# Experts of a routed layer with a fixed plan of blocks in place of branches

## The chip, the cores and the metric

The program runs on one core of one Trainium2 chip. The metric is the time of one execution on the device in microseconds (us), as a median over runs. The engines are named as in the profile: PE is TensorE (matmuls; PEld is its weight load), DVE is VectorE, ACT is ScalarE, POOL is GpSimd, SP is SyncE, which here does nothing but issue transfers.

## The reference, cut to what matters

The layer mixes 2048 tokens (attention and a convolution), then routes each token to two of 32 experts, and ends with a gated embedding. The change lies in the experts:

```
def expert_block(args):
    xb, e = args                                  # 128 rows of one expert
    hdn = jax.nn.silu(xb @ w1[e]) * (xb @ w3[e])  # 1024 -> 512
    return hdn @ w2[e]                            # 512 -> 1024
```

w1 and w3 are 1024 x 512, w2 is 512 x 1024, all in float32. How many rows an expert gets is known only once the router has run.

## The kernel before, in words

Every float32 operand of a large matmul is taken in two parts, high and low (`split`, L91 to L93): ACT copies the high part, a second engine subtracts it from the whole. A product is then three matmuls: high by high, high by low, low by high (`mm3`, L95 to L99). For a block of at most 64 rows the two parts of the rows lie side by side in one 128-column operand, so that two matmuls do (`both`, L1127).

The weights of an expert come in 12 pieces of 128 x 1024 (`unit`, L1080): SP loads a piece into `eraw` (9 buffers), ACT writes `ewh` and DVE or POOL `ewl` (15 buffers each). Pieces 0 to 3 serve the first half of the hidden columns (w1 and w3), 4 to 7 the second half, 8 to 11 are w2. `pull(n)` (L984) puts the next n pieces into the program; how many come at which place of an expert is written out in `PULLS`, 12 in all, and pieces 2, 6 and 10 are subtracted on POOL.

`pick` (L892) orders the experts by the number of their rows, large and small ones in turn, and writes for each of the 32 places which expert it is, its number of rows and of blocks. `moe` (L964) walks over the 32 places. Each has a first block of 128 rows, and what further blocks it has is settled by branches on the number of rows: none up to 128, a 64-row block up to 192, otherwise a 128-row block and more (`many`, L1001). A block: its rows are gathered by POOL (`gather`, L1092), transposed by PE and split (`turned`, L1100), multiplied with w1 and w3 (`products`, L1139, tile `ups`), gated (`gated`, L1164: silu on ACT, product on DVE), the hidden half transposed and split (`turn`, L1173, tiles `hps` and `hh`), multiplied with w2 (`down`, L1182, tile `yd`), copied and scattered by POOL. The second block of a place is set between the halves of the first. After the experts, `ple` (L1239) reads the scattered rows and makes the last products (tile `gps`) with 12 more pieces, pulled during the last expert.

Inside `moe` the order of instructions on each engine is that of the program (`manual_schedule`, L1022); nothing is moved by the compiler there.

Of the kernel before, what the change touches and what calls it, by code (L numbers as in the profile page):

```python
# [9 lines left out]
F32 = mybir.dt.float32  # L10
# [35 lines left out]
MOE_W = (9, 15)  # L46
POOL_UNITS = (2, 6, 10)
PULLS = (1, 1, 1, 2, 3, 2, 2)
# [3 lines left out]
HALF_FEW = 5  # L52
XT1_AT = 0
# [5 lines left out]
LEAD = (2, 200)  # L59

# [19 lines left out]
def AGAIN(nc, out, ps, sb):  # L80
    nc.gpsimd.tensor_copy(out, sb)


class K:
# [49 lines left out]
    def keep(self):  # L134
        """What lasts from the merge to the end."""
        cp = self.ctx.enter_context(self.tc.tile_pool(name="keep", bufs=1, reuse_waits="tile"))
        self.gl = cp.tile([P, NT, NG], F32, name="gl")
        self.nc.vector.memset(self.base, 0.0)
        self.dst = cp.tile([P, NBLK * NE], I32, name="dst")
        self.idx = cp.tile([P, NBLK * NE], I32, name="idx")  # L140
        self.slots = cp.tile([1, 3, NE], I32, name="slots")
        self.xp = self.ctx.enter_context(self.tc.tile_pool(name="xp", bufs=2, reuse_waits="tile"))

    def consts(self, cp):
# [24 lines left out]
        # brings in the table of the square root  # L169
# [383 lines left out]
    def attn_probs(self, h, g, Qt, Kt):  # L553
        """Unnormalized p0 - lam * (sum p0 / sum p1) * p1; what is missing, 1 / sum p0, goes into s0."""
# [262 lines left out]
    def route(self, q, L):  # L817
# [12 lines left out]
        def first(vals, top, k):  # L830
            """One-hot of the first place that holds the maximum."""
# [60 lines left out]
    def pick(self):  # L892
# [48 lines left out]
        V.tensor_copy(self.slots, vp[:1, :3, :])  # L941

# [1 line left out]
    def projected(self, t, pt, w, pool, tag, o):  # L944
        """Tile t of it, from units of [128, 1024] in two parts."""
# [9 lines left out]
    def project(self, parts):  # L955
        """The first half of the tiles, while the table is made."""
# [7 lines left out]
    def moe(self):  # L964
# [8 lines left out]
        self.ed = ctx.enter_context(tc.tile_pool(name="ed", bufs=2, space=PSUM, reuse_waits="tile"))  # L973
        engines = [ET.PE, ET.Activation, ET.DVE, ET.Pool, ET.SP]
        col = lambda t, e, b: t[:, b * NE + e : b * NE + e + 1]
        val = lambda i, e, lo, hi, eng=engines: nc.values_load(self.slots[0:1, i, e : e + 1], engines=eng, min_val=lo, max_val=hi)

        def rows(e, b):
            return self.gather(col(self.idx, e, b)) if e < NE else None

        W, src = {}, []
        self.last = W

        def pull(n, after=None):  # L984
            for _ in range(n):
                i = sum(len(w) for w in W.values())
                e, c = i // 12, i % 12
                if e > NE:
                    return
                if c == 0:  # L990
                    W[e] = []
                    if e == NE:
                        src[:] = halves(A["wpp"]) + halves(A["pT"][1]) + [A["wpg"][c, i] for c in range(2) for i in range(4)]
                    elif e:
                        i = val(0, e, 0, NE - 1, [ET.SP])
                        src[:] = [A["we"][bass.ds(i, 1), c] for c in range(12)]
                    else:
                        src[:] = [A["we"][0, c] for c in range(12)]
                W[e].append(self.unit(src[c], nc.gpsimd if c in POOL_UNITS else nc.vector, after))

        def many(e, w, n, xt, fill):  # L1001
            g = self.ep.tile([P, D], F32, name="g", tag="y")
            self.gather(col(self.idx, e, 2), g)
            self.block(w, xt, col(self.dst, e, 1), fill)
            with tc.If(n > 2 * P):
                self.turned(g, True, xt[3])
                with tc.If(n > 2 * P + FEW) as full:
                    self.block(w, xt, col(self.dst, e, 2), y=g)
                    with tc.If(n > 3 * P):
                        with tc.For_i(3, val(2, e, 0, NBLK), 1) as i:  # L1010
                            b = i * NE + e
                            self.gather(self.column(self.idx, b, "ix"), g)
                            self.block(w, self.turned(g, True, xt[3]), self.column(self.dst, b, "dx"), y=g)
                with full.Else():
                    self.block(w, xt, col(self.dst, e, 2), y=g, few=True)

        self.ctx.enter_context(tc.manual_schedule(engines={ET.SP}))
        xt, xt1 = (self.turned(x, more=i == 1) for i, x in enumerate(self.first))
        pull(EARLY)
        pull(12 - EARLY, self.gathered)  # L1020
        xs0 = rows(1, 0)
        with tc.manual_schedule(engines=set(engines)):  # L1022
            for e in range(NE):
                w = W[e]
                h0 = self.gated(self.raised(w, xt, 0, self.ups("eu")), "hd")
                u1 = self.ups("eu")
                fill = lambda i: self.products(w, xt, 1, u1, 0, i)
                pull(PULLS[0])
                n = val(1, e, 0, S)
                with tc.If(n > P) as more:  # L1030
                    if e % 2:
                        x = self.ep.tile([P, D], F32, name="g", tag="y")
                        xt1 = self.turned(self.gather(col(self.idx, e, 1), x), more=True)
                    with tc.If(n > P + FEW) as full:  # L1034
                        many(e, w, n, xt1, fill)
                    with full.Else():
                        self.block(w, xt1, col(self.dst, e, 1), fill, few=True)
                with more.Else():
                    for i in range(2):
                        fill(i)  # L1040
                def also(at):
                    nonlocal xt1
                    if e % 2 and e + 1 < NE and at == XT1_AT:
                        xt1 = self.turned(xs1, more=True)

                def between(n):
                    pull(PULLS[5 + n])
                    if n == 0:
                        also(3)

                t0 = self.turn(h0, self.halves())
                pull(PULLS[1])
                self.products(w, xt, 1, u1, 1, 0)
                also(0)
                self.products(w, xt, 1, u1, 1, 1)
                h1 = self.gated(u1, "hd")
                pull(PULLS[2])
                yd = self.yds()
                self.down(w, yd, 0, 0, t0)
                also(1)  # L1060
                t1 = self.turn(h1, self.halves())
                pull(PULLS[3])
                self.down(w, yd, 0, 1, t0)
                if e + 1 < NE:
                    xt = self.turned(xs0)
                also(2)
                xs0 = rows(e + 2, 0)
                if e % 2 == 0:
                    xs1 = rows(e + 2, 1)
                pull(PULLS[4])  # L1070
                self.lowered(w, yd, t1, col(self.dst, e, 0), pull=between)
                if e == 0:
                    pull(MOE_W[1] - 12 - PULLS[0])

# [5 lines left out]
    def unit(self, src, lo_eng=None, after=None):  # L1080
        """A [128, 1024] piece of a weight matrix in two parts."""
# [18 lines left out]
    def turned(self, x, more=False, into=None):  # L1100
        """The transpose of a [128, 1024] tile in two parts, [128, 8, 128] each; `more`: the high part of 64 rows
# [274 lines left out]
```

## Time and profile before

| what | us |
|---|---|
| median of 3 runs | 2954.33 |
| lowest and highest run | 2951.59, 2961.68 |
| span of the profiled execution, first to last instruction | 2960.1 |
| first matmul of the experts | 1727.9 |
| first matmul of the last stage's projection | 2712.6 |

The profiled execution has its span as its own time; what lies around a span is not listed, and the span lies inside the range of the runs. The experts take about a third of it. PE is busy for 92% of the span, DVE 69%, ACT 50%, POOL 24%; these shares are means over stages that have little in common.

### The profile page before, as it was taken

To read this page: it belongs to the slowest core of one execution; us is meant where nothing else is said; L and a number is where in the kernel's file an instruction comes from. 1 tells how busy PE (TensorE), PEld (TensorE's weight loads), DVE (VectorE), ACT (ScalarE), POOL (GpSimd) and SP (SyncE) were. 2 spreads that over 40 slices of the span, in tenths; PEclk is the share of its full clock that TensorE was granted. 3 is DMA by queue.
4 is the path that set the end of the run, shared out by engine and by line. 5 is a ranking of instruction groups with operands and counts; after the bars stand their busy time and mean duration, and the time that the engine had idled before them with its cause. 6 is when DMAs were issued, how large, how long until landed. Compare 5 with 4: busy or idle time off the path is not lost. (4 is left out here: it accounts for less than half of the span.)

```text
span 2960.1 us, 40065 instructions
## 1 busy us (share of the span) xinstructions
PE 2736.7 (92%) x14078; PEld 2282.7 (77%) x14078; DVE 2041.7 (69%) x2860; ACT 1474.9 (50%) x2712; POOL 722.3 (24%) x463
## 2 busy tenths in 40 slices
PE   7999999999999999999999989898888989888988
PEld 5888877997778788787898867676666767666776
DVE  6995249995878888657567456666667777776564
ACT  4233352335766667544444345555455656565443
POOL 2021130123111000001101134544335444452122
PEclk9999999999999999999999989999999999999999
DMA  5134443235243331456556366777767776876371
GB/s 189 60 107 142 159 147 104 93 114 196 81 132 89 104 112 53 160 184 214 168 170 206 122 238 243 265 287 259 252 223 274 276 283 236 293 274 244 125 246 56
DMA packets 180220, 531.52 MB, mean 180 GB/s; under 512 B 19185, under 2 KB 48641, under 8 KB 179361
## 3 DMA queue, kind: packets, MB, share of 16 engines
q1 hardware_dynamic: 135536, 397.02, 39.9%
q0 software_dynamic: 25904, 92.45, 8.5%
q10 hardware_dynamic: 18432, 37.76, 3.4%
q8 instruction: 177, 2.90, 0.4%
q14 instruction: 171, 1.39, 0.1%
HBM read 424.66 MB, written 102.50 MB: 178 GB/s over the span
## 5 line engine op out<-in xcount | busy, mean ns | idle before, releaser
L93 DVE TENSOR_TENSOR ewl<-eraw,ewh 128x1024 fp32r<-128x1024 f32 x365 | 597.2, 1665 | 94.4 <-ACT ewh L92 88.5
L92 ACT ACTIVATE ewh<-eraw 128x1024 fp32r<-128x1024 f32 x464 | 474.1, 1065 | 54.0 <-PE mps L98 24.9
L387 DVE SCALAR_TENSOR_TENSOR co<-cb,pvt,co 128x1024 f32<-128x1024 f32 x240 | 313.6, 1345 | 1.6
L93 POOL TENSOR_TENSOR ewl<-eraw,ewh 128x1024 fp32r<-128x1024 f32 x99 | 253.8, 2563 | 185.4 <-ACT ewh L92 183.0
L1146 PE MATMUL ups<-ewh,xt 128*128 128x512 f32 x592 | 250.0, 422 | 40.3 <-issue 38.6
L1147 PE MATMUL ups<-ewl,xt 128*128 128x512 f32 x592 | 244.5, 413 | 0.9 <-DVE ewl L93 0.5
L97 PE MATMUL ps<-uh,wh 128*128 128x512 f32 x576 | 232.0, 405 | 4.4 <-ACT uh L92 4.4
L586 DVE TENSOR_REDUCE nm<-sc 128x1 f32<-128x512 f32 (+3 forms) x320 | 185.3, 606 | 66.1 <-PE sc L583 51.6
L98 PE MATMUL ps<-ul,wh 128*128 128x512 f32 x576 | 227.9, 397 | 1.1 <-POOL ul L93 1.1
L99 PE MATMUL ps<-uh,wl 128*128 128x512 f32 x576 | 227.2, 396 | 0.0
L1146 PEld LDWEIGHTS ups<-ewh,xt 128*128 128x128 f32 x592 | 119.0, 201 | 71.9 <-issue 46.0
L97 PE MATMUL ps<-wh,uh 128*128 128x384 f32 x512 | 173.0, 338 | 0.0
L99 PE MATMUL ps<-wh,ul 128*128 128x384 f32 x512 | 172.1, 336 | 0.0
L98 PE MATMUL ps<-wl,uh 128*128 128x384 f32 x512 | 172.0, 336 | 0.0
L1144 PE MATMUL ups<-ewh,xt 128*128 128x512 f32 x592 | 167.5, 406 | 3.7 <-issue 3.7
L97 PE MATMUL mps<-ewh,mh 128*128 128x256 f32 x512 | 150.3, 294 | 4.1 <-ACT mh L92 4.1
L403 POOL DMA_DIRECT2D G<-sg x64 | 35.1, 549 | 457.3 <-ACT sg L402 325.2
L98 PE MATMUL mps<-ewl,mh 128*128 128x256 f32 x512 | 145.8, 285 | 0.0
L99 PE MATMUL mps<-ewh,ml 128*128 128x256 f32 x512 | 145.2, 285 | 0.0
L1147 PEld LDWEIGHTS ups<-ewl,xt 128*128 128x128 f32 x592 | 119.3, 202 | 25.5 <-DVE ewl L93 1.0
L430 POOL TENSOR_TENSOR qn<-qk,qk_std 128x1024 f32<-128x1024 f32 x16 | 44.6, 2785 | 380.7 <-DVE qk_std L189 363.8
L1204 POOL DMA_INDIRECT Y<-y,dst x48 | 72.3, 1507 | 266.3 <-POOLq L1034 188.3
(340 smaller groups left out, 7238.5 us busy)
## 6 DMA issues: line engine op xcount, KB each, us to landing
eraw<-in_we SPq DMA_DIRECT2D x384, 512.0 KB, 7.3
G<-sg POOLq DMA_DIRECT2D x64, 256.0 KB, 2.7
eraw<-in_wac SPq DMA_DIRECT2D x32, 512.0 KB, 4.3
ga<-G SPq DMA_DIRECT2D x32, 512.0 KB, 5.1
eraw<-in_wo SPq DMA_DIRECT2D x32, 512.0 KB, 3.7
ys<-Y SPq DMA_DIRECT2D x32, 512.0 KB, 8.2
wraw<-in_wqkv SPq DMA_DIRECT2D x16, 768.0 KB, 4.2
wraw<-in_wg SPq DMA_DIRECT2D x20, 512.0 KB, 3.9
```

The lines of the kernel that those rows point to most:

```text
L92: nc.scalar.activation(hi, x, AF.Copy)
L93: (lo_eng or nc.vector).tensor_tensor(lo, x, f32(hi), ALU.subtract)
L97: nc.tensor.matmul(ps, lh, rh, start=start, stop=False)
L98: nc.tensor.matmul(ps, lh, rl, start=False, stop=False)
L99: nc.tensor.matmul(ps, ll, rh, start=False, stop=stop)
L387: nc.vector.scalar_tensor_tensor(acc, cb[:, i : i + HALF], wi, acc, ALU.mult, ALU.add)
L430: nc.gpsimd.tensor_tensor(qn.rearrange("p t (s d) -> p t s d", d=HD), qk.rearrange("p t (s d) -> p t s d", d=HD), r.unsqueeze(3).to_broadc ...
L586: nc.vector.tensor_reduce(nm[:, qi, m, c : c + 1], sc[:, :w], AX.X, ALU.max, negate=True)
L1144: self.nc.tensor.matmul(ps, xt[1][:, k, :], wk[0], start=False, stop=k == NK - 1)
L1146: self.nc.tensor.matmul(ps, xt[0][:, k, :], wk[0], start=k == 0, stop=False)
L1147: self.nc.tensor.matmul(ps, xt[0][:, k, :], wk[1], start=False, stop=False)
L1204: nc.gpsimd.indirect_dma_start(out=self.Y[:, :], out_offset=bass.IndirectOffsetOnAxis(ap=dst[R], axis=0), in_=y[R], in_offset=None)
```

## The change

A list `PLAN` says for each place in the order by rows which blocks it gets: five places two blocks of 128 rows (one of them a further 64), eleven 128 and 64, nine 128, seven 64. The blocks are put into the program without branches. An expert with more rows than its place holds is done once more, all its blocks, in a loop behind the others (`rest`), whose weights are loaded and split there for each block; `pick` writes a flag and, per place, the number of blocks to be redone. The order of PE's work is now written in steps: `X` transposes rows, `U(j, f, g)` is half `g` of the product for hidden half `f`, `T` turns a hidden half, `DN` is the product with w2. In a place with two blocks the steps of both are interleaved. Weight pieces are no longer pulled at fixed places: `did` keeps a count of PE's and DVE's time and pulls from that, and `U` and `DN` pull whatever they need that is not there yet. All pieces are subtracted on DVE; the buffers of `ewh` and `ewl` are 14 each.

```diff
-MOE_W = (9, 15)
-POOL_UNITS = (2, 6, 10)
-PULLS = (1, 1, 1, 2, 3, 2, 2)
+MOE_W = (9, 14)
+FULL, PART = P, FEW
+PLAN = [[FULL, FULL], [FULL, FULL, PART]] + [[FULL, FULL]] * 3 + [[FULL, PART]] * 11 + [[FULL]] * 9 + [[PART]] * 7
+SLOTS = [PLAN[s // 2 if s % 2 == 0 else NE - 1 - s // 2] for s in range(NE)]
+UNIT_US = 1.25
...
+        def pull(after=None):
+            nonlocal pulled, dve
...
+            W[e].append(self.unit(src[c], None, after))
+            pulled += 1
+            dve = max(dve, pe) + UNIT_US
+
+        def did(us):
+            nonlocal pe
+            pe += us
+            while dve <= pe and pulled < 12 * NE + 12 and (pulled < MOE_W[1] or pulled - MOE_W[1] in last):
+                pull()
+
+        def small(us):
+            nonlocal dve
+            dve = max(dve, pe) + us
...
+        def X(j):
...
+            j.xt = self.turned(j.x, j.few)
+            rows(j.k + 2)
+            small(0.64 if j.few else 1.28)
+            did(0.5 if j.few else 0.87)
+
+        def U(j, f, g):
+            while pulled <= 12 * j.e + 4 * f + 2 * g + 1:
+                pull()
...
+            if j.ends:
+                for c in range(2):
+                    last[12 * j.e + 4 * f + 2 * g + c] = True
+            if g == 1:
+                j.h = self.gated(j.u, j.few)
+                small(1.1 if j.few else 0.4)
+            did(1.82 if j.few else 2.72)
+
+        def T(j):
+            j.ht = self.turn(j.h, j.few)
+            small(0.4)
+            did(0.2)
+
+        def DN(j, f):
+            while pulled <= 12 * j.e + 8 + 2 * f + 1:
+                pull()
...
+                did(0.91 if j.few else 1.36)
...
+            for i, g in enumerate(groups):
+                nxt = groups[i + 1][0] if i + 1 < len(groups) else None
+                a = g[0]
+                X(a)
+                U(a, 0, 0)
+                held()
+                held = lambda: None
+                if len(g) == 2:
+                    b = g[1]
+                    X(b)
+                    U(a, 0, 1)
+                    U(b, 0, 0)
+                    T(a)
+                    a0 = a.ht
+                    U(b, 0, 1)
+                    U(a, 1, 0)
+                    T(b)
+                    b0 = b.ht
+                    U(a, 1, 1)
+                    a.ht = a0
+                    DN(a, 0)
+                    U(b, 1, 0)
+                    T(a)
+                    U(b, 1, 1)
+                    b.ht = b0
+                    DN(b, 0)
+                    X(nxt)
+                    T(b)
+                    DN(a, 1)
+                    DN(b, 1)
+                else:
+                    U(a, 0, 1)
+                    if nxt and not (a.few and nxt.few):
+                        X(nxt)
+                    U(a, 1, 0)
+                    T(a)
+                    U(a, 1, 1)
+                    DN(a, 0)
+                    X(nxt)
+                    T(a)
+                    held = lambda a=a: DN(a, 1)
+            held()
+            while pulled < 12 * NE + 12:
+                pull()
+            self.rest()
```

`last` holds the pieces whose last reader is already in the program. `gated` follows the second half of a product at once; `held` puts the last step of a place with one block behind the first step of the next place. Outside the experts, `ple` no longer has POOL copy 64 rows of every second tile, and `pick` gains 32 memsets and five small operations on DVE.

## Rows read from the trace of the kernel before

**Rows 1.** View by stretches; after the engines: granted clock, DMA share, GB/s.

```profile
core 0: us, PE busy (x) PEld busy (x) DVE busy (x) ACT busy (x) POOL busy (x), PEclk, DMA share, GB/s
...
1728.00:2708.00 980.00, 867.69 (x3800) 674.63 (x3801) 668.43 (x630) 550.90 (x800) 423.99 (x228) 0.94 0.73 262
```

**Rows 2.** PE's waits, 1728 to 2708 us: total, times, longest.

```profile
PE ups L1146 <- issue: 38.6, 16, 3.3
PE ups L1130 <- issue: 32.1, 11, 3.5
...
PE ups L1146 <- ACT ewh L92: 1.6, 1, 1.6
```

**Rows 3.** Groups by line and form, 1720 to 2720 us.

```profile
L93 DVE TENSOR_TENSOR ewl<-eraw,ewh 128x1024 fp32r<-128x1024 f32 x297 | 514.2, 1767 | 48.1 <-ACT ewh L92 42.3
L92 ACT ACTIVATE ewh<-eraw 128x1024 fp32r<-128x1024 f32 x396 | 402.4, 1067 | 2.5 <-DMA eraw<-in_we 2.3
L93 POOL TENSOR_TENSOR ewl<-eraw,ewh 128x1024 fp32r<-128x1024 f32 x99 | 253.8, 2563 | 185.4 <-ACT ewh L92 183.0 <-ACTq L1030 1.4
L1146 PE MATMUL ups<-ewh,xt 128*128 128x512 f32 x592 | 250.0, 422 | 40.3 <-issue 38.6 <-ACT ewh L92 1.6
...
L1131 PE MATMUL ups<-ewl,xt 128*64 128x512 f32 x192 | 84.4, 462 | 3.8 <-issue 3.8
```

**Rows 4.** Timeline of PE, 2333 to 2381 us: start, length, instruction, [idle before].

```profile
2333.74 1.08 PE L1144 MATMUL ups<-ewh,xt 128*128 128x512 f32 x4
2334.65 0.39 PE L97 MATMUL yd<-ewh,hh 128*128 128x512 f32 x1
2334.88 0.39 PE L98 MATMUL yd<-ewl,hh 128*128 128x512 f32 x1
...
2336.02 0.38 PE L1177 MATMUL hps<-cst,hd 128*128 128x128 f32 x2
...
2337.63 1.04 PE L1111 MATMUL tps<-cst,xs 128*128 128x128 f32 x8
2338.43 0.47 PE L97 MATMUL yd<-ewh,hh 128*128 128x512 f32 x1
...
2372.88 0.62 PE L1130 MATMUL ups<-ewh,xt 128*128 128x512 f32 x1 [2.71 <-issue]
...
2375.86 0.63 PE L1133 MATMUL ups<-ewh,xt 128*128 128x512 f32 x1
2376.28 0.47 PE L1131 MATMUL ups<-ewl,xt 128*64 128x512 f32 x1
...
2378.21 0.39 PE L1130 MATMUL ups<-ewh,xt 128*128 128x512 f32 x1
...
2381.05 0.34 PE L1177 MATMUL hps<-cst,hd 64*128 64x64 f32 x2
```

**Rows 5.** Timeline of ACT, 2334 to 2380 us.

```profile
2334.85 0.38 ACT L1169 ACTIVATE hd<-ups 128x256 f32<-128x256 f32 x1 [1.05 <-PE ups L1144]
2335.13 1.05 ACT L92 ACTIVATE ewh<-eraw 128x1024 fp32r<-128x1024 f32 x1
2336.49 0.38 ACT L92 ACTIVATE hh<-hps 128x256 fp32r<-128x256 f32 x1 [0.30 <-ACT ewh L92]
...
2338.66 1.08 ACT L92 ACTIVATE xt<-tps 128x512 fp32r<-128x512 f32 x2
...
2379.91 0.42 ACT L1169 ACTIVATE hd<-y 64x256 f32<-64x256 f32 x1 [0.80 <-DVE y L1137]
```

**Rows 6.** Timeline of DVE, 2336 to 2338 us.

```profile
2336.22 1.23 DVE L93 TENSOR_TENSOR ewl<-eraw,ewh 128x1024 fp32r<-128x1024 f32 x1 [0.53 <-ACT ewh L92]
2337.36 0.42 DVE L93 TENSOR_TENSOR hh<-hps,hh 128x256 fp32r<-128x256 f32 x1
```

**Rows 7.** Waits of SP's queue: total, times, longest.

```profile
SPq L1084 <- DVE ewl L93: 432.9, 219, 31.1
```

**Rows 8.** Transfers, 1728 to 2708 us: count, KB each, us to landing.

```profile
eraw<-in_we SPq DMA_DIRECT2D x375, 512.0 KB, 7.4
```

More of the change, by code (lines that the diff above doesn't have):

```diff
@@ L940, in pick @@
             nc.tensor.matmul(vp[:1, c, :], vals[:NE, c : c + 1], own[:NE, :], start=c == 0, stop=c == 2)
-        V.tensor_copy(self.slots, vp[:1, :3, :])
+        V.tensor_copy(self.slots[:, :2, :], vp[:1, :2, :])
+        caps, again, over = new("caps", NE), new("again", NE), new("over", 1)
+        for e in range(NE):
+            V.memset(caps[:1, e : e + 1], float(sum(SLOTS[e])))
+        V.tensor_tensor(again[:1], vp[:1, 1, :], caps[:1], ALU.is_gt)
+        V.tensor_tensor(again[:1], again[:1], vp[:1, 2, :], ALU.mult)
+        V.tensor_copy(self.slots[:, 2, :], again[:1])
+        V.tensor_reduce(over[:1], again[:1], AX.X, ALU.max)
+        V.tensor_copy(self.over, over[:1])
     def projected(self, t, pt, w, pool, tag, o):
@@ L978, in rows @@
-        def rows(e, b):
-            return self.gather(col(self.idx, e, b)) if e < NE else None
-        W, src = {}, []
+        W, src, last = {}, [], {}
         self.last = W
[L984 to L996, printed above, removed]
-                    else:
-                        src[:] = [A["we"][0, c] for c in range(12)]
-                W[e].append(self.unit(src[c], nc.gpsimd if c in POOL_UNITS else nc.vector, after))
@@ L1001, in many @@
[L1001 to L1015, printed above, removed]
@@ L1017, in moe @@
-        self.ctx.enter_context(tc.manual_schedule(engines={ET.SP}))
[L1018 to L1031, printed above, removed]
-                        x = self.ep.tile([P, D], F32, name="g", tag="y")
[L1033 to L1073, printed above, removed]
@@ new lines, in did, with __init__ @@
+        def did(us):
[6 more added lines that the diff above has]
+            dve = max(dve, pe) + us
+        class Job:
+            def __init__(j, k, e, b, few, ends):
+                j.k, j.e, j.b, j.few, j.ends = k, e, b, few, ends
+                j.R = slice(0, FEW if few else P)
+                j.done = False
@@ new lines, in U @@
+        def U(j, f, g):
+            while pulled <= 12 * j.e + 4 * f + 2 * g + 1:
+                pull()
+            w = W[j.e]
+            if g == 0:
+                j.u = self.eu.tile([P, 512], F32, name="ups", tag="eu")
+            if j.few:
+                self.products_few(w, j.xt, f, j.u, g)
+            else:
+                for i in range(2):
+                    self.products(w, j.xt, f, j.u, g, i)
+            if j.ends:
[5 more added lines that the diff above has]
+            did(1.82 if j.few else 2.72)
@@ new lines, in T @@
+        def T(j):
[5 more added lines that the diff above has]
+                pull()
+            if f == 0:
+                j.yd = [self.ed.tile([P, 512], F32, name="yd", tag="ed") for _ in range(2)]
+            y = self.ep.tile([P, D], F32, name="y", tag="y") if f else None
+            for n in range(2):
+                self.down(W[j.e], j.yd, f, n, j.ht, j.few)
+                if f:
+                    yn = y[j.R, n * 512 : (n + 1) * 512]
+                    if j.few:
+                        self.total(yn, j.yd[n])
+                        small(0.68)
+                    else:
+                        nc.scalar.copy(yn, j.yd[n])
+                if n and j.ends:
+                    for c in range(2):
+                        last[12 * j.e + 8 + 2 * f + c] = True
+                did(0.91 if j.few else 1.36)
+            if f:
+                self.scatter(y, col(self.dst, j.e, j.b), j.R)
@@ new lines, in moe @@
+        jobs, groups = [], []
+        for e, plan in enumerate(SLOTS):
+            new = []
+            for b, n in enumerate(plan):
+                new.append(Job(len(jobs), e, b, n == PART, False))
+                new[-1].x = None
+                jobs.append(new[-1])
+            new = [new[:2], new[2:]] if len(new) > 2 else [new]
+            new[-1][-1].ends = True
+            groups += new
+        for j, x in zip(jobs, self.first):
+            j.x = x
+        self.ctx.enter_context(tc.manual_schedule(engines={ET.SP}))
@@ new lines, in moe @@
+        with tc.manual_schedule(engines=set(self.engines)):
+            X(jobs[0])
+            X(jobs[1])
+            for _ in range(EARLY):
+                pull()
+            for _ in range(EARLY, 12):
+                pull(self.gathered)
+            held = lambda: None
[5 more added lines that the diff above has]
+                held()
+                held = lambda: None
+                if len(g) == 2:
[21 more added lines that the diff above has]
+                    DN(b, 1)
+                else:
+                    U(a, 0, 1)
[10 more added lines that the diff above has]
+            while pulled < 12 * NE + 12:
+                pull()
+            self.rest()
@@ L1171, in gated, with turn @@
         return hd
-    def turn(self, hd, ht, few=False):
+    def turn(self, hd, few):
         n = FEW if few else P
+        ht = self.ep.tile([P, 4, P], F32R, name="hh", tag="hh", bufs=3)
         ps = self.et.tile([P, 512], F32, name="hps", tag="et")[:, : 2 * n]
```

167 lines of the change are left out of this document (86 added, 81 removed).

## The prediction

> **What bounds the kernel now.** I read the stretch of the experts first, since nothing else but two small places changes: first matmul at 1727.9 us, last one at about 2711 (table above), so 983 us of the span of 2960.1. The view by stretches [rows 1] shows PE busy for 868 of 980 us there, at a mean granted clock of 0.94, DVE busy for 668 and ACT for 551, DMA at 0.73. That puts PE first, but a busy matmul is not a matmul at its pace, so I count PE's work at full pace. In the timeline of PE [rows 4] two neighbouring 512-column matmuls start 0.23 us apart (2334.65, 2334.88; over a longer row 0.228). The counts [rows 3] give the blocks: 592 / 16 = 37 of 128 rows, 192 / 16 = 12 of 64 rows. A 128-row block is 72 matmuls, 16.4 us, with 0.80 us for eight transposes of its rows (2337.63 to 2338.43) and 0.28 for the two turns of its hidden half: 17.5 us. A 64-row block is 48 matmuls, 11.0 us, and 1.2 beside them: 12.2. In all 37 x 17.5 + 12 x 12.2 = 794 us. The other 189 us of the 983 are lost, and the list of PE's waits [rows 2] says to what: 50 waits in thirteen rows, 114 us, of which the first two, products that wait on "issue" right behind a branch, are 71; the longest row of weights (ewh) is 1.6 us. [...] So: PE-bound, with a tax at the branches, and weights that are always ready, because the 12 pieces of an expert are split while the expert before it runs.
>
> **What the change removes.** No branch stands between blocks: the 71 us go, and with them most other waits. Seven places get one 64-row block where a 128-row block stood. The 37 blocks are 32 first ones and five more; with the twelve of 64 rows that is what the plan holds for the large experts; by the inputs the seven smallest experts have 28 to 43 rows. So all fit, and the loop behind is skipped. PE's work becomes 30 x 17.5 + 19 x 11.9 (a 64-row block's transposes now have half the columns) = 751 us, 43 less.
>
> GpSimd splits nothing any more. DVE takes those 99 pieces, 99 x 1.23 = 122 us by an undisturbed piece [rows 6], but its own 297 pieces have a mean of 1767 ns now [rows 3] and would take 1.23, 160 us back. DVE then has 396 x 1.23 = 487 us and some 180 of small work, under 751: not a bound by its sum. Nor is DMA: a piece lands in 7.4 us [rows 8], and SP's longest waits are for DVE to free a buffer [rows 7], so nine pieces stay ahead whatever follows.
>
> **What it adds: weights split just in time.** The order of pieces is no longer written out, but planned by `did`. It adds a step's time to `pe` and issues pieces while `dve <= pe`; but `pull` sets `dve = max(dve, pe) + 1.25`, so after one piece `dve` is past `pe` and the loop ends. One step brings at most one piece, and a [128] expert has 11 steps for 12 pieces, of which the short turns bring none. DVE's time that passes unused while the 14 buffers are full (until the second job of a pair has begun) is never made up. What `did` left out is then issued by the `while` ahead of `U` and `DN`, right before the matmuls that read it. I followed this bookkeeping through all 32 places: of the 372 pieces behind the first expert's, 263 come by those `while` loops, at 133 points, and from the fifth place on nearly every step of a first job has one. The twelve for the last stage all come after the last expert.
>
> A piece so placed stands in ACT's and DVE's queues behind the gate, the turn or the transposes of the PE step just before it, and these wait for that step's end. PE then waits for the whole way round. From rows of the same sequence: a product's last matmul ends at 2334.82, its gate starts on ACT at 2334.85, the high part of the next piece at 2335.13 [rows 5], its low part on DVE at 2336.22 and it ends at 2337.45 [rows 6]. Without the wait the first matmul with a low part would start at 2334.88; with some 0.1 us to the start that is 2.7 us. The others follow:
> - behind the turn of a hidden half (its matmul at 2336.02 [rows 4], ACT at 2336.49 [rows 5]): 2.8; behind the transposes of rows (0.80 us on PE [rows 4], then the second of the two xt on ACT, 1.08 for both [rows 5]): 2.9;
> - behind a gate of 64 rows, which goes ACT, DVE, ACT (from the next slot at 2378.21 [rows 4] to the end of the second ACT step at 2380.33 [rows 5], then a piece as above): 4.2;
> - where `DN` needs its second piece after three matmuls, 0.4 more: 3.1, or 5.1 behind a 64-row gate;
> - where only the second of two pieces is late, the first's five matmuls cover 1.14: 1.7 behind a turn (1.8 with the shorter 64-row steps), 3.0 behind a 64-row gate;
> - four pieces at once, the third needed first: 2.8 + 2 x 1.14 (a DVE piece lets the next operation start 1.14 later, 2336.22 to 2337.36 [rows 6]) = 5.1.
>
> The 133 points by kind: `DN` 24 x 3.1 + 6 x 5.1 = 105; second half of the second product, behind a turn, 17 x 2.8 + 13 x 1.8 = 71; four at the start of a pair 14 x 5.1 = 71, four other starts 11; behind transposes 25 x 2.9 = 72; second product behind a gate 4 x 2.7 + 4 x 4.2 + 7 x 3.0 = 49; second half of the first product, 8 that earlier work hides and 3 that it doesn't, 8; `DN` of the second half 4 x 2.8 = 11. Sum 398 us, over 125 waits that are felt. The bounds: if sixteen of the 4.2 and 5.1 kinds and every second piece overlapped more than I see, 2.4 a wait, 300; if ACT's pieces, 1067 ns each [rows 3], never overlapped with DVE's, 3.8, 475.
>
> **The clock.** No row of before has PE waiting this often. At the 1.05 us a wait that the stage shows now, 125 waits cost 131 us. Bounds: nothing if pauses of 3 us were too short, and 125 x 1.7 = 213 if each were followed by 3.4 us at the lower level, as the one at 2372.88 is (eight matmuls 0.2 us late each). I take 131, since some of today's waits of 2 to 3 us are followed by it and some are not. [...]
>
> **Small ones.** Seven turns in 64-row experts wait about 1.0 us for their gate (the turn at 2381.05 less 2378.21, less 1.85 of the step between): 7. The start, where the first pieces arrive as now: 5. Last stage: pieces 1 to 3 of its twelve and the skipped loop's branch stand ahead of its first matmul, about 5 and 2.4 (38.6 / 16) [rows 2]: 8 on the path; before they were ready. It also has 14 buffers for 15; the copies for 64 rows on GpSimd go: nothing, between -3 and +5. The routing's 32 memsets and five small operations on DVE: 0 to 4, 2 taken, as DVE has idle places there.
>
> **Sum.** 751 + 398 + 131 + 7 + 5 = 1292 for 983: +309; +8 +2 gives +319. The span of 2960.1 becomes 3279; the runs' median is 2954.3, 6 below the span, so about **3274 us**.
>
> **Rivals.**
> - *Pieces are early after all* (other side). If ACT and DVE come to their pieces before the gate or turn in front is due, because those stand further apart in the queues than I count, the 398 + 131 shrink to a few waits: 751 + 7 + 5 + some 40 = 803, and 2960 - 180 + 10 = 2790. The point from which it decides: without the two terms the change wins 220 - 10 = 210 us, so it breaks even at 1.7 us a wait, the clock's share included. For it: today's list of waits has almost none for weights. Against: today pieces of the next expert fill the whole of an expert's time, and DVE is seen to sit behind its gates and turns in program order, with pieces ready.
> - *The waits, but little clock*: 300 to 398 lost and 0 to 40 of clock: 3050 to 3190. For: 2-us waits of before often leave the clock up.
> - *The clock falls at every wait and PE's steps stretch with it*: 475 + 213 or more: 3370 to 3500. For: the pause at 2372.88 and what follows it [rows 4]; against: the stage's mean of 0.94 [rows 1].
> - *A wash*: the waits only as dear as today's branches, 2950 to 2960. This needs those 1.7 us a wait; no row has so short a way round.
>
> **Chances and range.** Forecast with its own range (3190 to 3360) 0.60; waits with little clock 0.15; clock at every wait 0.10; early pieces 0.13; a wash 0.02. The measurement tells about 0.3% (the runs lie within 0.35%). Faster 0.13, same 0.02, slower 0.85. The range takes the forecast, nearly all of the second and half of the third case: 3080 to 3430.
>
> **What would show it.** In the changed kernel's stage: PE's waits with ACT's ewh and DVE's ewl as releasers, over a hundred, near 3 us; ewl near 1.23 us in the mean; clock near 0.85; no wait on "issue" inside; GpSimd without subtractions; stage near 1290. If the list of waits has few rows for ewl, the count of late pieces is wrong; if the waits are there but near 1.5 us, the way round is.

## The result, and the profile after

The changed kernel takes **3353.72 us** (median of four runs, 3351.26 to 3362.66) where the kernel before, on the same chip, takes 2955.52: ratio 1.135, interval 1.1329 to 1.137. It is slower by 398 us. The forecast was 3274, range 3080 to 3430: right in its sign and inside its range, 80 us low.

The profiled execution has a span of 3360.9 us (before: 2960.1). The experts' first product starts at 1727.5 us and their last product with w2 ends at 3098.7: a stage of 1371 us, where it was 983 and 1292 was forecast. Behind it come 262 us (3360.9 less 3098.7), before 249 (2960.1 less 2711). So 388 of the 401 us lie in the stage, and none ahead of it. The view by stretches, for the stage (it answers to [rows 1]):

```profile
core 0: us, PE busy (x) PEld busy (x) DVE busy (x) ACT busy (x) POOL busy (x), PEclk, DMA share, GB/s
1727.00:3099.00 1372.00, 1027.41 (x3644) 711.70 (x3644) 626.50 (x732) 555.63 (x792) 104.44 (x94) 0.83 0.53 178
```

PE does less (3644 instructions where it had 3812) and is busy for longer, at a clock of 0.83 instead of 0.94; DVE and ACT are busy for less than half the stage, and DMA's share falls from 0.73 to 0.53. By its sum no engine fills the stage: PE waits for 345 us of it and has part of its work at a lower clock. The list of PE's waits (what is waited for: us in total, times, longest us), which was headed by products behind branches [rows 2]:

```profile
PE ups L1254 <- ACT ewh L90: 142.0, 75, 3.4
PE ups L1255 <- DVE ewl L91: 61.8, 89, 1.1
PE yd L95 <- ACT ewh L90: 38.4, 27, 1.6
PE yd L96 <- DVE ewl L91: 23.7, 38, 1.0
PE hps L1279 <- DVE xt L91: 18.9, 14, 1.9
PE ups L1240 <- DVE ewl L91: 17.3, 17, 2.6
PE yd L1239 <- ACT ewh L90: 16.7, 6, 2.8
PE hps L1279 <- DVE hd L1271: 10.2, 3, 9.2
```

All 285 waits of the list come to 345 us; 267 of them, 314 us, are for weights (before: 2 of 50, 2.1 us). A late place (one where a `while` issues pieces right ahead of the matmuls that read them, the prediction's "points") shows as two waits: for the high part from ACT, then, one matmul later, for the low part from DVE. How one looks is seen in the timelines of PE, ACT and DVE (start, duration, instruction; in brackets the idle time before it and its releaser):

```profile
3084.38 1.08 PE L1257 MATMUL ups<-ewh,xt 128*128 128x512 f32 x4
3086.87 0.50 PE L95 MATMUL yd<-ewh,hh 128*128 128x512 f32 x1 [1.42 <-ACT ewh L90]
3088.13 0.50 PE L96 MATMUL yd<-ewl,hh 128*128 128x512 f32 x1 [0.76 <-DVE ewl L91]
3088.47 0.40 PE L97 MATMUL yd<-ewh,hh 128*128 128x512 f32 x1
3088.70 0.40 PE L95 MATMUL yd<-ewh,hh 128*128 128x512 f32 x1
...
3093.09 0.51 PE L95 MATMUL yd<-ewh,hh 128*128 128x512 f32 x1 [1.48 <-ACT ewh L90]
3094.34 0.79 PE L96 MATMUL yd<-ewl,hh 128*128 128x512 f32 x1 [0.76 <-DVE ewl L91]
3094.94 0.63 PE L97 MATMUL yd<-ewh,hh 128*128 128x512 f32 x1
3095.36 0.63 PE L95 MATMUL yd<-ewh,hh 128*128 128x512 f32 x1
```

```profile
3085.49 0.38 ACT L1270 ACTIVATE hd<-ups 128x256 f32<-128x256 f32 x1 [3.23 <-PE ups L1257]
3085.77 1.99 ACT L90 ACTIVATE ewh<-eraw 128x1024 fp32r<-128x1024 f32 x2
```

```profile
3085.91 0.42 DVE L1271 TENSOR_TENSOR hd<-hd,ups 128x256 f32<-128x256 f32 x1 [2.39 <-ACT hd L1270]
3086.85 2.36 DVE L91 TENSOR_TENSOR ewl<-eraw,ewh 128x1024 fp32r<-128x1024 f32 x2 [0.52 <-ACT ewh L90]
```

The product ends at 3085.46. ACT has been idle for 3.23 us, because the gate stands first in its queue and waits for that end; the piece behind it begins at 3085.77, its low part at 3086.85, and PE's first matmul with that at 3088.13: 2.67 us behind the product's end, where the forecast had worked out 2.7. The lone matmul between the two waits lasts 0.50 us instead of the 0.23 from one to the next in a row (3088.47 to 3088.70). After the next place the matmuls stand 0.42 us apart (3094.94 to 3095.36): the granted clock is 0.50 from 3094.90 to 3097.40, where it is 1.00 from 3088.10 to 3091.20.

The groups by form, for DVE's and ACT's share of the pieces (count, busy us, mean ns, idle time before it and its releasers; the answer to [rows 3]):

```profile
L91 DVE TENSOR_TENSOR ewl<-eraw,ewh 128x1024 fp32r<-128x1024 f32 x384 | 454.1, 1222 | 122.3 <-ACT ewh L90 107.3 <-DMA eraw<-in_we 11.9
L90 ACT ACTIVATE ewh<-eraw 128x1024 fp32r<-128x1024 f32 x384 | 385.0, 1050 | 7.3 <-DMA eraw<-in_we 6.8 <-PE ups L1242 0.3
```

A piece costs DVE 1222 ns, as forecast, and hardly one waits for its transfer (6.8 us in all on ACT, 11.9 on DVE).

### The profile page after: what moved, and what is told of

It is laid out like the page before. It is cut to its first block, busy times and chain, and to the rows that moved or that the text cites. A ratio compares the mean times of both kernels' runs of the same rounds, so it can differ in the third digit from the quotient of the medians.

```text
span 3360.9 us, 38599 instructions
## 1 busy us (share of the span) xinstructions
PE 2897.9 (86%) x13910; PEld 2320.1 (69%) x13911; DVE 2009.8 (60%) x3006; ACT 1483.5 (44%) x2708; POOL 386.6 (12%) x311
## 5 line engine op out<-in xcount | busy, mean ns | idle before, releaser
L91 DVE TENSOR_TENSOR ewl<-eraw,ewh 128x1024 fp32r<-128x1024 f32 x464 | 550.8, 1221 | 173.1 <-ACT ewh L90 157.8
L1254 PE MATMUL ups<-ewh,xt 128*128 128x512 f32 x480 | 245.1, 511 | 142.0 <-ACT ewh L90 142.0
L1255 PE MATMUL ups<-ewl,xt 128*128 128x512 f32 x480 | 254.9, 531 | 61.8 <-DVE ewl L91 61.8
L1254 PEld LDWEIGHTS ups<-ewh,xt 128*128 128x128 f32 x480 | 115.5, 241 | 180.4 <-ACT ewh L90 162.8
L91 DVE TENSOR_TENSOR hh<-hps,hh 128x256 fp32r<-128x256 f32 (+1 forms) x98 | 36.4, 371 | 240.7 <-ACT hh L90 239.5
L90 ACT ACTIVATE hh<-hps 128x256 fp32r<-128x256 f32 (+1 forms) x98 | 33.6, 343 | 319.1 <-PE hps L1279 319.1
L1257 PE MATMUL ups<-ewh,xt 128*128 128x512 f32 x480 | 159.4, 462 | 0.0
L95 PE MATMUL yd<-ewh,hh 128*128 128x512 f32 x240 | 112.9, 470 | 38.5 <-ACT ewh L90 38.4
L1257 PEld LDWEIGHTS ups<-ewh,xt 128*128 128x128 f32 x480 | 116.6, 243 | 31.0
```

What stands on the lines that cost most here:

```text
L90: nc.scalar.activation(hi, x, AF.Copy)
L91: (lo_eng or nc.vector).tensor_tensor(lo, x, f32(hi), ALU.subtract)
L95: nc.tensor.matmul(ps, lh, rh, start=start, stop=False)
L1254: self.nc.tensor.matmul(ps, xt[:, k, :P], wk[0], start=k == 0, stop=False)
L1255: self.nc.tensor.matmul(ps, xt[:, k, :P], wk[1], start=False, stop=False)
L1257: self.nc.tensor.matmul(ps, xt[:, k, P:], wk[0], start=False, stop=k == NK - 1)
```

## What makes up each stage

One table for the kernels below, all in us, by one working. Stage: first to last matmul of the experts. Work: as in the prediction, 794 for the blocks of before and 751 for those of the change. Waits: the sum of PE's list (their number). Weights: those of them for ewh or ewl. Clock: PE's busy time times one less the granted clock, from the view by stretches; the view has the clock in two digits, which leaves this column and the rest open by some 5 us. Rest: what is left.

| kernel | stage | work | waits | weights | clock | rest |
|---|---|---|---|---|---|---|
| before | 983 | 794 | 114 (50) | 2 | 52 | 23 |
| after | 1371 | 751 | 345 (285) | 314 | 175 | 100 |
| e1_ahead | 978 | 751 | 143 (69) | 2 | 58 | 26 |
| e2_carry | 890 | 751 | 77 (47) | 3 | 33 | 29 |
| e3_half | 1040 | 751 | 165 (142) | 108 | 70 | 54 |
| e4_nolow | 1114 | 751 | 240 (145) | 213 | 61 | 62 |
| e5_before_dve | 931 | 794 | 88 (43) | 2 | 25 | 24 |
| e6_carry_pool | 967 | 751 | 142 (68) | 3 | 50 | 24 |
| e7_carry_serial | 944 | 751 | 112 (121) | 24 | 33 | 48 |
| e8_carry_moved | 861 | 751 | 61 (60) | 3 | 16 | 33 |
| e10_before_late | 1195 | 794 | 247 (138) | 118 | 95 | 59 |
| e11_filled | 1310 | 851 | 249 (274) | 218 | 96 | 114 |

The rest is 23 to 33 where few waits are for weights, and grows with them: by the 0.27 us that the matmul behind a wait lasts longer (0.50 less 0.23), 285 waits make 77 of the 100 of after. Counted over the trace wait by wait (what the matmuls on both sides of a wait take beyond the spacing in a row at the same clock) it is 78 us for the 285 waits of after and 12 for the 50 of before; the 22 and 11 that are left stay open. Counted in the same way, the matmuls that stand 0.43 us apart instead of 0.24 cost after 169 us, near the 175 of the column. The work of e11_filled has 438 recorded matmuls more, 100 us.

## The experiments

The theory: pieces are issued right ahead of the matmuls that read them, and PE waits for the way round through the queues of ACT and DVE; the clock falls by these waits. The rivals: the new order of PE's steps is itself slow; DVE is full; the clock falls for another reason.

**Pieces ahead of time by the bookkeeping** (e1_ahead). A piece costs the planner nothing, so that it issues all that the buffers hold.

```diff
-UNIT_US = 1.25
+UNIT_US = 0.0
```

> UNIT_US 0: a piece goes into the program as soon as its buffer is free there; by the bookkeeping no piece of the experts is left to the loops ahead of U and DN. Theory (late pieces cost the 400 us): PE's waits on ewh and ewl go, stage of the experts 1371 -> about 830 us (751 of work, some 40 waits of 1 us for turns that now stand behind two pieces, their clock, the start), whole time 3354 -> about 2805. Rival 1 (the interleaved order of PE's steps sets gate and use too close together): stage stays above 1200, time above 3180. Rival 2 (DVE is the bound since it took GpSimd's pieces): stage stays above 1250, DVE's idle time shrinks instead.

Measured: 2954.22 us, ratio to before 0.9984 (0.9969 to 0.9998). The 314 us of waits for weights are gone, and 400 of the time with them, but it is not the 2805 expected. A new wait has taken part of it:

```profile
PE hps L1279 <- DVE xt L91: 91.2, 24, 6.8
PE ups L1239 <- DVE xt L91: 14.6, 12, 3.0
```

Now the pieces stand ahead of the small work in DVE's queue, and the turn of a hidden half waits for it, 91 us in 24 places. One of them, on DVE and on PE:

```profile
2156.85 2.36 DVE L91 TENSOR_TENSOR ewl<-eraw,ewh 128x1024 fp32r<-128x1024 f32 x2 [0.53 <-ACT ewh L90]
2159.12 1.28 DVE L91 TENSOR_TENSOR xt<-tps,xt 128x512 fp32r<-128x512 f32 x2
2159.86 0.47 PE L1279 MATMUL hps<-cst,hd 64*128 64x64 f32 x2 [4.89 <-DVE xt L91]
```

Too early has a price as well.

**Pieces ahead, but spread** (e2_carry). The planner keeps the time that it owes, instead of forgetting it when PE's count has passed DVE's; no piece is late, and none comes much too early.

```diff
-            dve = max(dve, pe) + UNIT_US
+            dve = dve + UNIT_US
```

> pull adds 1.25 to dve instead of to the larger of dve and pe, so that unused DVE time is made up; no piece left to the loops, but pieces come less bunched than with UNIT_US 0. Theory (late pieces): stage about 810 us, time about 2785, at or a little under the run with UNIT_US 0. Rival 1 (order of steps): above 3180. Rival 2 (DVE bound): above 3200.

Measured: 2866.05 us, ratio 0.9695 (0.9674 to 0.9716). One line of bookkeeping is worth 488 us (3353.72 less 2866.05) and turns the change into a gain. Its stretch, and what heads its waits:

```profile
1719.00:2609.00 890.00, 813.71 (x3644) 620.56 (x3645) 621.97 (x743) 560.92 (x803) 113.63 (x93) 0.96 0.80 278
```

```profile
PE hps L1279 <- DVE xt L91: 45.8, 17, 3.7
```

Same blocks, same order of PE's steps, 622 us of DVE where there were 626: the interleaved order and DVE's load are not what makes the changed kernel slow. It misses the 2785 expected by 81 us, for turns that wait and for a clock of 0.96.

**About a third of the late places** (e3_half). By the bookkeeping 48 places are late instead of 133.

```diff
-UNIT_US = 1.25
+UNIT_US = 0.6
```

> UNIT_US 0.6: by the bookkeeping 63 pieces at 48 places come late instead of 263 at 133. Theory (late pieces, price by kind as in the prediction: 14 starts of a pair about 3.9, 3 behind a turn 1.8, 25 at DN 2.4, 6 behind transposes 1.8): 131 us of waits and 48 x 1.4 of clock, stage 751 + 131 + 67 + 40 = 990, time about 2970. Rivals 1 and 2: no change beyond 30 us from 3354.

Measured: 3027.97 us (one run), 58 more than expected, the stage 1040.

```profile
1725.00:2766.00 1041.00, 876.91 (x3644) 639.47 (x3644) 619.40 (x732) 553.37 (x793) 120.72 (x93) 0.92 0.70 235
```

Against the 890 with none late, 48 places cost 150 us, 3.1 each; 133 cost 481, 3.6 each (clock included). The time goes with the number of late places, at prices that lie 16% apart.

**Half of the way round** (e4_nolow). The low part of the experts' weights is left out: no subtraction on DVE, and the matmuls that read it read the high part again. The pieces are as late as in the changed kernel.

```diff
-            W[e].append(self.unit(src[c], None, after))
+            W[e].append(self.unit(src[c], None, after, e < NE))
...
+        if high:
+            nc.scalar.activation(wh, raw, AF.Copy)
+            return wh, wh
```

> The changed kernel with the low part of the experts' weights left out: no subtraction on DVE for them, the matmuls that read the low part read the high part again, as many matmuls as before. Theory (PE waits for the way round over ACT and DVE): each of 125 waits is shorter by DVE's step, about 1.1 us, and by 1.45 at the 14 places of four pieces, 140 us, and the clock gives 30 to 90 back: stage 1140 to 1200, time 3120 to 3180; what waits are left end with ACT's ewh. Rival 1 (order of steps, gates): less than 50 us. Rival 2 (DVE bound): all of it goes, stage near 830.

Measured: 3096.07 us (one run).

```profile
1725.00:2838.00 1113.00, 874.07 (x3644) 631.67 (x3644) 176.73 (x347) 553.82 (x790) 88.78 (x93) 0.93 0.64 219
```

```profile
PE ups L1257 <- ACT ewh L1210: 144.0, 81, 3.4
```

DVE has only 177 us to do, and the waits for ACT's part stay as they were (142.0 us in 75 in the changed kernel, 144.0 in 81 now); only the second wait of each place is gone. So DVE's load is refuted as the cause a second time. The time is 24 us below the range expected, by the clock: 0.93 instead of 0.83, its share 61 instead of 175, 114 less where 30 to 90 were expected. The places are as many, but each has one pause instead of two with a lone matmul between.

**The kernel before without GpSimd's subtractions** (e5_before_dve). The part of the change that the prediction had costed by DVE's sum alone.

```diff
-POOL_UNITS = (2, 6, 10)
+POOL_UNITS = ()
```

> The kernel before with all pieces subtracted on DVE. Theory (before is bound by PE and its branches, DVE has room): DVE's mean for a piece falls from 1767 to about 1225 ns, its total hardly moves, the time falls by 0 to 25 us: 2930 to 2958. Rival (GpSimd's hold on DVE was on the path): 2900 or less, which would be a gain that the change kept. Rival 2 (DVE becomes the bound): above 2970.

Measured: 2911.41 us, ratio 0.9845 (0.9825 to 0.9866): 43 us of gain, more than the 0 to 25 of the theory and less than the 55 of the rival, so that neither holds as it was put.

```profile
L93 DVE TENSOR_TENSOR ewl<-eraw,ewh 128x1024 fp32r<-128x1024 f32 x392 | 459.3, 1218 | 33.2 <-ACT ewh L92 30.5
```

A piece takes DVE 1218 ns, where it took 1767 with GpSimd beside it [rows 3]; with a third more pieces DVE is busy for 615 us in place of 668 [rows 1], and the waits, 88 for 114, and the clock, 25 for 52, shrink with it.

**GpSimd's subtractions back in the better planner** (e6_carry_pool), the same part from the other side, on top of e2_carry.

```diff
-            W[e].append(self.unit(src[c], None, after))
+            W[e].append(self.unit(src[c], nc.gpsimd if c in (2, 6, 10) else nc.vector, after))
```

> The kernel with the carried DVE time, pieces 2, 6 and 10 subtracted on GpSimd as before the change. Theory (one GpSimd piece of 2.5 us holds DVE for as long): 96 pieces less on DVE free 118 us there and its own get slower by some 150, gates come later, waits of turns and of late pieces grow: 2866 -> 2890 to 2960. Rival (DVE's queue is what delays the gates, so relief helps): 2830 to 2860.

Measured: 2939.25 us (one run), inside the range of the theory and 73 more than e2_carry.

```profile
L91 DVE TENSOR_TENSOR ewl<-eraw,ewh 128x1024 fp32r<-128x1024 f32 x296 | 481.3, 1658 | 219.8 <-ACT ewh L90 218.4 <-issue 0.5
L91 POOL TENSOR_TENSOR ewl<-eraw,ewh 128x1024 fp32r<-128x1024 f32 x99 | 252.8, 2555 | 383.0 <-ACT ewh L90 320.7 <-issue 53.6 <-PE hps L1279 6.4
```

DVE is busy for longer with 296 pieces (481 us) than with all (465 in e2_carry's row by form). Piece by piece, the 124 of DVE's 296 that run at the same time as one of GpSimd's take 2268 ns in the mean, the other 172 take 1218 and at most 1284. In the trace of before 84 of DVE's 297 pieces begin while GpSimd has one in work: each of the 84 ends 1.08 to 1.09 us behind the end of GpSimd's, 1.70 to 3.43 us after its own start, where the 115 that run beside none take 1.22.

**The interleaving taken back** (e7_carry_serial). e2_carry with the two blocks of a place one after the other.

```diff
-                    X(b)
                     U(a, 0, 1)
-                    U(b, 0, 0)
-                    T(a)
-                    a0 = a.ht
-                    U(b, 0, 1)
+                    X(b)
                     U(a, 1, 0)
-                    T(b)
-                    b0 = b.ht
+                    T(a)
                     U(a, 1, 1)
...
                     DN(a, 0)
-                    U(b, 1, 0)
                     T(a)
+                    U(b, 0, 0)
+                    DN(a, 1)
+                    U(b, 0, 1)
+                    U(b, 1, 0)
+                    T(b)
                     U(b, 1, 1)
```

> The kernel with the carried DVE time, the two blocks of a place one after the other instead of interleaved; by the bookkeeping nine pieces at six places come late. Theory (late pieces were the whole of the loss, interleaving only covers gates): 64-row turns lose cover, 18 times about 1 to 2 us with clock, some relief elsewhere: 2866 -> 2860 to 2920. Rival (interleaving was itself a cost): below 2850.

Measured: 2923.56 us (one run), 58 more than e2_carry and 4 above the range expected. Its list has 121 waits for 47, 112 us for 77; 24 us of them are for weights, since in this order a few pieces are late again. Of the 54 us that the stage is longer (944 less 890), late pieces take 21 of waits and some 6 beside them (24 waits at 0.27); about 27 are left for the order. So the interleaving is a gain, not the trouble.

**Transposes and turns set apart** (e8_carry_moved). In e2_carry a turn often comes just behind the transposes of the next rows, and both take their PSUM tile from the same two buffers. In a pair the second turn goes into the middle of `DN`, in a single block the transposes go behind the turn.

```diff
-                    T(b)
-                    DN(a, 1)
+                    DN(a, 1, lambda: T(b))
...
                     U(a, 0, 1)
-                    if nxt and not (a.few and nxt.few):
-                        X(nxt)
                     U(a, 1, 0)
                     T(a)
                     U(a, 1, 1)
+                    if nxt and not (a.few and nxt.few):
+                        X(nxt)
```

> The kernel with the carried DVE time, and two steps moved: in a pair the turn of the second block's last hidden half stands inside the first block's last product, behind the next rows' transposes and one half product, in a single place the next rows' transposes stand behind the last quarter of the product instead of ahead of the turn. Theory (what is left there, 46 us of waits of turns put down to the split of the transposed rows, is a PSUM bank of the two that transposes and turns share): most of it goes with its clock, 2866 -> 2815 to 2825. Rival (these turns wait for their 64-row gate): little changes where the turn has as much cover as before, 2850 to 2870.

Measured: **2838.95 us**, ratio 0.9603 (0.9574 to 0.9631), the fastest of all and 115 us ahead of the kernel before.

```profile
1725.00:2585.00 860.00, 800.56 (x3644) 607.14 (x3643) 621.28 (x742) 559.75 (x801) 115.22 (x93) 0.98 0.83 287
```

```profile
PE hps L1280 <- DVE xt L91: 19.4, 13, 1.8
```

The turn's wait falls from 45.8 to 19.4 us and the clock rises to 0.98. The gain is 27 us where 41 to 51 were expected.

**Late pieces in the kernel before** (e10_before_late). e5_before_dve with branches and order as they were, and only the places of the pieces moved.

```diff
+                if e:
+                    pull(4)
...
-                pull(PULLS[0])
+                if e:
+                    pull(PULLS[0])
...
-                if e == 0:
-                    pull(MOE_W[1] - 12 - PULLS[0])
+            pull(12)
```

with `PULLS = (8, 0, 0, 0, 0, 0, 0)`.

> The kernel before with all pieces subtracted on DVE (2911 us, an earlier run), branches and order of PE's work as they were; the pieces are moved alone: from the second expert on, four come right ahead of the expert's first product and eight right behind it (none is left in the places ahead), and the last stage's twelve come behind the experts. Theory (a piece issued right ahead of its matmuls sends PE the whole way round, whatever else the kernel does): 31 starts at some 3.1 us, 16 waits of about 1 us where the four come behind the gate or transposes in part, and about 40 us by a lower clock: about 3060, and waits for ewh and ewl head PE's list. Rival (late pieces hurt only in the interleaved order without branches): 2911 to 2930, and the list is headed by the products behind branches as before.

Measured: 3177.31 us, ratio 1.0739 (1.0718 to 1.0761): 266 more than e5_before_dve, where the theory had 149 and the rival 0 to 19.

```profile
PE ups L1148 <- ACT ewh L92: 89.9, 48, 3.7
PE hps L1179 <- DVEq L1033: 52.7, 16, 3.7
PE ups L1132 <- issue: 31.5, 11, 4.1
PE ups L1149 <- DVE ewl L93: 28.4, 40, 0.8
```

```profile
2326.04 9.17 DVE L93 TENSOR_TENSOR ewl<-eraw,ewh 128x1024 fp32r<-128x1024 f32 x8 [0.52 <-DMA eraw<-in_we]
2335.42 0.66 PE L1179 MATMUL hps<-cst,hd 128*128 128x128 f32 x2 [3.72 <-DVEq L1033]
```

The rival falls: late pieces hurt this kernel as they hurt the other. The waits for weights are 118 us, near the 112 that 31 x 3.1 + 16 make. What the expectation had left out is what the eight pieces do to those behind them: DVE is held for 9.17 us, its branch (L1033) stands behind, and the turn waits 3.72 us for that at 2335.42, 52.7 in all; another 27.4 us of the turn wait for DVE's hd (2.9 in e5_before_dve). The clock's share rises from 25 to 95.

**PE kept at work in the pauses** (e11_filled). The changed kernel, with matmuls whose results are overwritten.

```diff
+        def busy(ps, x):
+            wh = W[(pulled - 3) // 12][(pulled - 3) % 12][0]
+            for _ in range(FILL):
+                nc.tensor.matmul(ps, x, wh[:, :512], start=True, stop=True)
...
+            if pulled <= 12 * j.e + 4 * f + 2 * g + 1 and g == 0:
+                busy(j.u, j.xt[:, 0, :P])
```

> The changed kernel with six more 512-column matmuls ahead of every late first half of a product and every late first half of a product with w2, 76 of the 133 late places; they read operands that are there already and write the bank which the product then starts afresh, so their results are overwritten. PE does 456 matmuls more (about 104 us at 0.228 us each), all of it inside pauses of some 3 us. Theory of the clock (the stage's 0.83 is the price of PE's pauses): the pauses filled, the granted clock rises towards 0.9, and the time falls by 50 to 90 us, to 3265 to 3305, although PE does more. Rival (the clock falls with something else, the load of the other engines say): the clock stays at 0.83 and the time at 3354 or above, up to 3400 where the extra matmuls at half pace stick out of the pauses.

Measured: 3298.16 us, ratio to before 1.1147 (1.1127 to 1.1167): 56 us less than the changed kernel, although PE has 438 more matmuls on record.

```profile
1724.00:3034.00 1310.00, 1061.53 (x4082) 736.31 (x4082) 626.15 (x731) 555.02 (x791) 101.31 (x93) 0.91 0.56 187
```

```profile
PE ups L1264 <- ACT ewh L91: 85.8, 75, 2.0
```

The clock rises from 0.83 to 0.91 and its share falls by 79 us (175 to 96). The waits for weights are 96 us less (314 to 218), which the 100 us of added work fill, so that the weights come no sooner. DVE's and ACT's busy times are those of the changed kernel (626 and 555 us). So in this kernel the lower clock is the price of PE's pauses, and not of what the other engines do.

## Why the prediction came out as it did

**The mechanism was right.** Late pieces are what the change costs, with the clock that falls by them: the list of waits has the forecast releasers, and with the pieces in time the same blocks in the same order take 2866 (e2_carry). Late pieces, with what eight at once hold up on DVE, slow the kernel before by 266 us (e10_before_late). The rival "pieces are early after all" falls, and so do the two on the change's order and on DVE's load.

**Term by term**, against the 1292 forecast for the stage (1371 measured, 79 more):

| term | forecast | measured | difference |
|---|---|---|---|
| waits for weights | 398 | 314 + 267 x 0.27 = 386 | -12 |
| clock | 131 | 175 | +44 |
| turns and gates | 7 | 31 + 18 x 0.27 = 36 | +29 |
| start and what no list shows | 5 | 23 | +18 |

- *The way round* was forecast at 2.7 us for a piece behind a gate and took 2.67; the sum over the kinds came out within 12 us. That is not errors which cancel. Laid over the order of steps, the trace gives for each kind (waits, and 0.27 for each), forecast in brackets: first `DN` of a block 97 (105), second half of the second product 66 (71), four pieces at the start of a pair 66 (71), other starts 12 (11), behind transposes 78 (72), second product behind a gate 49 (49), second half of the first product 4 (8), `DN` of the second half 11 (11).
- *The clock* was sized by 1.05 us for each of 125 late waits, an estimate of the author: 6% of PE's 868 us, by the mean granted clock of 0.94 [rows 1], over the 50 waits of before. No run shows it as the price of one wait; they show the clock's sum over a stage. In this kernel that rate comes out of it: 142 us more of clock than with no late piece (175 less 33 in e2_carry) over 133 places is 1.07. But it is no constant, and that it fitted is in part luck: by the same sum it is 0.77 in e3_half (70 less 33, 48 places) and 0.21 in e4_nolow (61 less 33, 133 places). What failed in the term is that only late places were charged. The stage without a late one still loses 33 us, since turns wait there too. The upper bound of 213 puts 3.4 us at the lower level behind every wait. That level is a granted clock of 0.50, as the view of before has it from 2374 to 2376, behind the pause at 2372.88. It does not come behind every wait: of the 19 waits of 2 to 3 us in the kernel before, 13 have it within the 3.4 us behind them and 6 do not; in the changed kernel 81 of the 285 matmuls behind a wait are at it within 0.1 us of their start (15 of 50 before), and those behind the wait at 3088.13 are at full pace (3088.47 to 3088.70).
- *Turns and gates, and the start*, were the steps with the largest relative error. Of the 31 us of waits, 9.2 are one wait at the start (3.9 in the kernel before), where DVE takes eight pieces ahead of the first gate:

```profile
1736.85 10.14 DVE L91 TENSOR_TENSOR ewl<-eraw,ewh 128x1024 fp32r<-128x1024 f32 x8 [4.70 <-ACT ewh L90]
1747.93 0.69 PE L1279 MATMUL hps<-cst,hd 128*128 128x128 f32 x2 [9.25 <-DVE hd L1271]
```

  The seven late gates of 64-row experts that the prediction charged are not there (1.0 us in the two other waits for `hd`). In their place 14 turns wait 18.9 us for DVE's `xt`, which the prediction put at nothing. The new order sets the transposes of the next rows right ahead of a turn, and both take their PSUM tile from the same two buffers. It is not the interleaving that does it: without it (e7_carry_serial) 27 turns still wait 31.5 us for `xt`. e8_carry_moved, which sets the two apart, takes that wait from 45.8 to 19.4 us; that it is the shared buffers was the reason for the edit, and the edit's effect bears it out, but no run gave the turn buffers of its own.
- *The last term*: of the 189 us that the stage before lost, 114 are waits and 52 the clock (first row of the table); the other 23 were dropped in the forecast's sum without a reason, and 23 or more are there in every kernel of the table.
- *Last stage*: 13 us more instead of 8. The list of waits just behind the stage has the two that were forecast, at 3.5 and 2.5 us:

```profile
PE pps L95 <- ACT ewh L90: 3.5, 1, 3.5
PE pps L95 <- ACTq L1157: 2.5, 1, 2.5
```

They make 6 of the 13. The granted clock is 0.84 in the 31 us behind the stage (3098.7 to 3130), where it had been 1.00 (2711 to 2742): of PE's 23.0 us there that is 4 more. The last 3 stay open. *Routing*: 2 us forecast, none seen (the first product starts 0.4 us earlier). In all 79 + 5 - 2 = 82, and 3279 + 82 = 3361, the span.

**Where the 2790 of the early case went wrong.** The prediction gave the change without late pieces 2790 us. Three versions without them give 2954, 2866 and 2839. The 803 us of that sum took 40 for waits and clock, where e2_carry has 110 (77 + 33) and 29 beside. What the sum left out are the waits of PE's turns: in e1_ahead pieces that are too early hold up the small work for which a turn waits, and in e2_carry 17 turns still wait 45.8 us for `xt`.

**GpSimd's part** was costed as 38 us less on DVE and nothing on the path. It is worth 43 us of the time by itself (e5_before_dve) and 73 in the better planner (e6_carry_pool). What it is worth in the changed kernel itself, where DVE is idle for half of the stage, no run shows.

## What to carry to other kernels

Where engines work through their queues in order, as ACT and DVE do here (ACT idle for 3.23 us ahead of the gate at 3085.49, with two pieces behind it), a helper's work that is issued "just when it is needed" comes a whole trip round too late (2.67 us in the rows above): it sits behind the very step that it should overlap. A planner that places such work should carry its debt forward (here one `max` cost 488 us), count the late pieces at build time, and leave room ahead of the short steps for which the main engine turns round. Compare the waits of the main engine with its busy time before looking at any engine's sum.

## What the runs showed of the chip

- In these runs two pauses with a lone matmul between them cost more clock than one: 0.83 with 285 waits of 1.2 us in the mean (345 / 285), 0.93 with 145 of 1.7 (240 / 145, e4_nolow), though the places are the same. The sum of the pauses differs too; but with nearly the same sum, 249 us in 274 waits cost 96 us of clock (e11_filled) and 240 in 145 cost 61 (e4_nolow). Matmuls of no use in the first pause of 76 places bring the clock from 0.83 to 0.91 and make the kernel 56 us faster.
- A subtraction on GpSimd (2555 ns) stretches those on DVE that run beside it from 1218 to 2268 ns in the mean (e6_carry_pool; 1658 over all), so that handing a quarter of the pieces to GpSimd gives DVE more to do, not less (481 us of subtractions for 465 in e2_carry).
